# Layer 1 of a two-layer trunk: h as one joined tile per stream, the context's x0 added by DMA, the gate's products in the output projection

## The chip, the cores and the metric

One core of one Trainium2 chip. The time is device microseconds of one execution of the program on that core; the kernel was run three times, and a separate execution was recorded by the hardware profiler. Engines: PE (matrix products), ACT and DVE (elementwise work, also out of PSUM), POOL (elementwise work in SBUF), SP (which here issues all DMAs).

## The reference

Two layers over 256 latent tokens (x) and 256 context tokens (ctx), 2048 features, everything float32. Cut to what matters:

```python
for l in range(2):
    shift, scale, gate = split(silu(c) @ w_mod[l] + b_mod[l], 3)          # for x
    shift_c, scale_c, gate_c = split(silu(c_ctx) @ w_mod[l] + b_mod[l], 3)  # for ctx
    h   = rmsnorm(x, g_pre[l]) * (1 + scale) + shift
    h_c = rmsnorm(ctx, g_pre[l]) * (1 + scale_c) + shift_c
    proj, proj_c = h @ w_in[l], h_c @ w_in[l]        # au av ag q k v bg cx cg
    y = concat(gelu(au) * spatial_mix(gelu(av)) * silu(ag),
               attention(rope(q), [ctx keys, rope(k)], [ctx values, v], sink) * silu(bg),
               (real 2-D DFT of cx, then a linear map) * silu(cg))
    x_new = x + gate * rmsnorm(y @ w_out[l], g_post[l])
    if l == 0:
        ctx = ctx + gate_c * (the same for proj_c, with attention among ctx alone)
    x = x_new
return x
```

In layer 1 the context is used for its keys and values alone; all other products are of the latents.

## The kernel before, in words

**Products.** Every operand of a product is split exactly into a high part in float32r and a low part (operand minus high part), and a product is three matmuls: hi times hi, hi times lo, lo times hi (`mm3`, lines 383 to 386). Weights come in halves of a unit, 128 x 1024 each: SP loads `raw` (three buffers), ACT casts `whi` (L367), DVE subtracts `wlo` (L368), four buffers each; `Stream.next` keeps three halves ahead of PE. The normalised input stands in feature-major tiles, one pair `hh[k]`, `hl[k]` of 128 x 512 per k tile of 128 features: high and low part, columns 0 to 255 the latents (stream 0), 256 to 511 the context (stream 1).

**Units.** `tunit(n)` makes 128 output columns for n tokens: 16 k tiles of three matmuls into one PSUM bank. In layer 0 n is 512, in layer 1 it is 256 (latents only), but for k and v. The order in a layer: av and the first two heads of au together, k tile by k tile (`start_av`, `start_au`), then units au (2), cx (4), ag (4), cg (4), k (2), v, q (8), bg (8); then the output projection, in layer 1 with tokens on partitions, 4 blocks of 512 columns by 16 k tiles by 2 token tiles (`finish`).

**Order of work.** PE runs its instructions in the order of the program. Work that comes back to PE after other engines is written as generators in `Later`: each yields a time to wait, in microseconds of PE's own matmuls, which `tick` counts after every k tile (0.324 for 256 columns, 0.648 for 512, 1.296 for a k tile of the last projection) and checks there; so a wait ends at the next k tile. On the other engines instructions are placed by priority, `low(n)` puts some n places back, and each engine then runs its own list in order. Fourier (`fourier`, waits YF), the spatial mix (`branch_a`), attention (`attention`, waits YQ, YA, YB) and the boundary are such generators.

**Modulation.** Most products of silu(c) and w_mod run on DVE in steps that `pace` gives out per half of a unit: RATE steps per two halves of the phase named. The last 32 steps, `mod_gate1`, are layer 1's gate: four blocks of 512 columns (tiles ctrh, ctrl, nstrh, nstrl), eight steps each, a step being one 512 KB load into `mraw` (two buffers) and two DVE operations (L245, L247), placed behind the newest weights' L368 and at `low(400)`. `gate1`, at the start of the output projection, sums each block over partitions by a matmul with ones (L260) and adds and multiplies rows of b_mod and g_post, loaded into `mraw` as well; `evac` multiplies the projection by it. `turn` brings x1 to tokens on partitions by PE transposes (L847) into the same two PSUM tiles.

**Boundary.** Between the layers `boundary(s, acc)` makes x1 = x0 + gate * y / rms(y) of one stream in place in `yo`, and 1 / rms of x1. For each k tile: DVE multiplies (L933), x0 is added (L934; DVE, or every second time POOL for the latents) from tiles loaded into `raw`, ACT squares (L937), and PE adds the squares over partitions (L944), two or four k tiles at a time. For the latents it runs at the end of layer 0's projection; for the context, within `boundary_ctx`, during layer 1's cx units, followed by the context's h (`make_h`). `gate` overwrites the context's columns of `yo[k]`, so it may not be placed before the context's h of tile k.

Of the kernel before, what the change touches and what calls it, by code (L numbers as in the profile page):

```python
# [27 lines left out]
def units():  # L28
    """(name, first column, columns, first k tile, k tiles): blocks of w_in of 128 x 2048 each."""
# [37 lines left out]
def trunk_kernel(ctx: ExitStack, tc: tile.TileContext, xT, xhalf, cT, wss, wsl, wmod, win, wout0, wout1, const, vec, rows,  # L67
# [24 lines left out]
    # ---- constants  # L92
# [17 lines left out]
    class low:  # L110
        """instructions that may wait for the next `n`."""
# [22 lines left out]
    # ---- modulation: columns [128, 16, stream] of scale, shift and gate  # L134
# [5 lines left out]
    def mod_cols(l, cb, ps8):  # L140
        """ps8 [128, 4, 2]: silu(c) @ w_mod for 512 columns of column block cb."""
# [12 lines left out]
    def mod_start(k0, nk):  # L154
        """scale and shift of k tiles k0 .. k0 + nk - 1 of layer 0 on the tensor engine: yields after
        each unit's products, and before the columns."""
# [39 lines left out]
    def mod_dve(l, cb, red):  # L196
        """red [128, 2, 16]: sums over the 32 partitions of each quadrant, transposed."""
# [38 lines left out]
    def mod_gate1():  # L236
        """products of silu(c) and the gate's columns of w_mod in layer 1, still to be summed over partitions."""
# [16 lines left out]
    def gate1():  # L254
        """(sum + b_mod) * g_post of layer 1's gate, on all partitions."""
        for c in range(4):
            r = sb([P, 2, 512], F32, "mraw", 2)
            DMA.dma_start(r, rows[None, :, c * 512:(c + 1) * 512].to_broadcast([P, 2, 512]))
            ps = ms_ps("gate")
            PE.matmul(ps, ones, g1[c], start=True, stop=True)  # L260
            V.tensor_tensor(out=g1[c], in0=r[:, 0], in1=ps, op=ALU.add)
            V.tensor_tensor(out=g1[c], in0=g1[c], in1=r[:, 1], op=ALU.mult)
            yield YT

    def mod_rest():
# [3 lines left out]
        while "acc" not in state:  # L269
# [6 lines left out]
    YF = [5.0, 2.8], [3.8, 3.4]  # L276
    RATE = dict(au0=2, cx0=2.2, ag0=2.2, cg0=2.2, k0=2, v0=2, q0=1.8, bg0=2.2, out0=2.8,
                k1=2.5, v1=2.5, q1=1, bg1=2.2)
    NEAR = [1] * 6 + [0] * 6 + [1, 2, 3]
    LOWC = 60  # L280
    YT = 2.0
    YH = 2.0
    NX = [4, 2]
    YX, YR = [1.0, 2.0], 0.8
    YQ, YA, YB = [5.5, 6.0], [10.0, 8.0], [3.8, 4.0]

    def pace():
        """steps of the modulation due per half of a unit, behind the latest weights on the vector engine."""
        state["owed"] += RATE.get(state["phase"], 0.0) / 2
        while state["owed"] >= 1:  # L290
            state["owed"] -= 1
            with low(LAG), tc.issue_after(W.last.ins):
                next(mods, None)

    # ---- work of other engines that hands products back to the tensor engine later
# [32 lines left out]
    # ---- weights: raw -> exact parts hi + lo, in halves of a unit, ahead of their use  # L328
# [59 lines left out]
    def part(w, c):  # L388
        """columns c of both parts; a part is a tile or a list of tiles side by side."""
# [19 lines left out]
    # ---- per-token reciprocal rms from sums over features  # L409
# [14 lines left out]
    def col_sums(ps, q, n, start=True, stop=True):  # L424
        """columns of ps: sums over the partitions of q [128, n * 128], one accumulation group."""
# [10 lines left out]
    # ---- streams in feature-major tiles  # L436
# [7 lines left out]

    def make_h(l, k, rb, streams):
        """h = x * rstd * gs + sh, as hi + lo; rb: rstd over the tokens of `streams`."""
# [6 lines left out]
        for s in streams:  # L453
            sl = slice(s * S, (s + 1) * S)
            first = A.activation(hh[k][:, sl], t[:, sl], AF.Identity, bias=sh[l][:, k, s:s + 1])  # L455
        for s in streams:
            sl = slice(s * S, (s + 1) * S)
            last = V.scalar_tensor_tensor(out=hl[k][:, sl], in0=t[:, sl], scalar=sh[l][:, k, s:s + 1],
                                          in1=hh[k][:, sl].bitcast(F32), op0=ALU.add, op1=ALU.subtract)
# [13 lines left out]
    def tunit(n, sl=None):  # L473
        """feature-major product of one unit of 128 columns: PSUM [128, n]."""
# [8 lines left out]
        return ps  # L483

# [10 lines left out]
    # ---- one layer, up to the inputs of the output projection  # L495
    def layer(l):
# [12 lines left out]
        # a_v (token-major) and two heads of a_u, k outermost  # L509
        av = [mm_ps("av") for _ in range(nt)]  # L510
        au = [mm_ps("au") for _ in range(2)]
        def start_av(k, ts):
            c = slice((k % 2) * 512, (k % 2 + 1) * 512)
            for t in ts:
                sl = slice(t * P, (t + 1) * P)
                mm3(av[t], (hh[k][:, sl], hl[k][:, sl]), part(avw, c), k == 0, k == KT - 1)

        def start_au(k):
            for j in range(2):
                c = slice((k % 4) * 256 + j * P, (k % 4) * 256 + (j + 1) * P)  # L520
                mm3(au[j][:, 0:n], part(auw, c), (hh[k][:, 0:n], hl[k][:, 0:n]), k == 0, k == KT - 1)
# [57 lines left out]
        # branch A  # L579
        def branch_a():  # L580
            vt = [w2k([P, 512]) for _ in range(nt)]
            ss = sb([P, 4], F32, "ss")
            for j in range(2):
                A.activation(ytmp(j), au[j][:, 0:n], AF.Gelu_apprx_tanh)
# [20 lines left out]
        # branch C  # L605
# [9 lines left out]
        def fourier(g, ps):  # L615
            """cos(2 pi t m / 256) is even in t around 128 and sin odd: positions t and 256 - t are added for the one
            and subtracted for the other, which leaves 128 rows each (position 128 in the sines' row of t = 0)."""
# [25 lines left out]
        # branch B  # L643
        def rope(hi, lo, ps):
            """x * cos + rot(x) * sin of the latents, and x of the context, as hi + lo."""
# [10 lines left out]
            if hi.shape[-1] > S:  # L656
                split_into(hi[:, CTX], lo[:, CTX], ps[:, S:T])
# [85 lines left out]
        for h in (2, 3):  # L743
            ps = tunit(n)
# [3 lines left out]
        for g in range(4):  # L748
            ps = tunit(n)
# [3 lines left out]
        for h in range(4):  # L753
            ps = tunit(n)
            gate(h, ps)
        state["phase"] = f"cg{l}"
        for g in range(4):
            ps = tunit(n)
# [6 lines left out]
        for j in range(2):  # L765
            ps = tunit(T)
            kt.append((sb([P, T], F32R, f"kt{j}"), sb([P, T], F32R, ("ws", "bsb")[j])))
            rope(*kt[j], ps)
# [3 lines left out]
        for k in range(KT):  # L772
# [3 lines left out]
            for t in range(4):  # L776
                ts = slice(t * P, (t + 1) * P)
                mm3(vps[t][:, 0:256], (hh[k][:, ts], hl[k][:, ts]), part(w, c), k == 0, k == KT - 1)
# [3 lines left out]
        for h in range(8):  # L782
            ps = tunit(n)
# [3 lines left out]
        for h in range(8):  # L787
            ps = tunit(n)
# [11 lines left out]
    # ---- output projection  # L800
# [7 lines left out]
    def out_proj():  # L808
# [14 lines left out]
        later.add(boundary(0, acc), 1.0)  # L823
# [271 lines left out]
```

## Time and profile before

| what | us |
|---|---|
| three runs: median (lowest, highest) | 1170.88 (1170.09, 1171.65) |
| span of the profiled execution | 1167.9 |
| PE busy in it | 1136.0 |
| DVE busy | 881.8 |
| ACT busy | 509.8 |
| POOL busy | 17.3 |

Stages of layer 1 in the profiled execution, read from the order of time: av and au about 757 to 808 us from the span's start, cx with the context's boundary 808 to 845, ag and cg 845 to 893, k and v 893 to 937, q to 1006, bg to 1064, output projection from there. The last product runs at 1158.65; the rest is the last evacuation and the stores.

How to read it: times are microseconds from the start of the span, L944 is line 944 of the kernel. A matmul's duration in the profile runs from its start to its modelled end and overlaps the next one's; its cost in a stream is the distance from start to start. float32 operands (not float32r) take two passes, so such a matmul appears as two. PEld is the load of a matmul's stationary operand. An idle time is put down to the engine or DMA that released it.

### The profile page before, as it was taken

To read this page: it belongs to the slowest core of one execution; us is meant where nothing else is said; L and a number is where in the kernel's file an instruction comes from. 1 tells how busy PE (TensorE), PEld (TensorE's weight loads), DVE (VectorE), ACT (ScalarE), POOL (GpSimd) and SP (SyncE) were. 2 spreads that over 40 slices of the span, in tenths; PEclk is the share of its full clock that TensorE was granted. 3 is DMA by queue.
4 is the path that set the end of the run, shared out by engine and by line. 5 is a ranking of instruction groups with operands and counts; after the bars stand their busy time and mean duration, and the time that the engine had idled before them with its cause. 6 is when DMAs were issued, how large, how long until landed. Compare 5 with 4: busy or idle time off the path is not lost.

```text
span 1167.9 us, 17483 instructions
## 1 busy us (share of the span) xinstructions
PE 1136.0 (97%) x6656; PEld 953.7 (82%) x6656; DVE 881.8 (76%) x1469; ACT 509.8 (44%) x914; POOL 17.3 (1%) x23
## 2 busy tenths in 40 slices
PE   3999999999999999999999999999999999999996
PEld 1466688888898888888888888889899999997885
DVE  5454498888988878798989886495896678888554
ACT  4222513322224667632533233365563278745442
POOL 0000000000000000000000000200000000000001
PEclk9999999999999999999999999999999999999998
DMA  9999765466665334455466665365656665688563
GB/s 339 378 387 357 254 196 166 145 202 193 200 200 178 105 114 136 134 175 173 158 199 209 205 216 162 109 207 173 205 158 205 203 200 178 195 269 244 190 187 120
DMA packets 73892, 234.32 MB, mean 201 GB/s; under 512 B 8528, under 2 KB 9680, under 8 KB 73808
## 3 DMA queue, kind: packets, MB, share of 16 engines
q1 hardware_dynamic: 73808, 233.21, 61.6%
q8 instruction: 52, 0.85, 0.3%
q14 instruction: 32, 0.26, 0.1%
HBM read 231.08 MB, written 2.10 MB: 200 GB/s over the span
## 4 chain that ended last, share of the span: by engine, by line
PE 92%; DVE 3%; DMA 2%; ACT 2%; issue 1%; POOL 0%; SPq 0%; DVEq 0%; ACTq 0%; POOLq 0%
PE ps_t L384 20%; PE ps_t L385 20%; PE ps_t L386 20%; PE ps_mod L172 3%; PE ps_av L384 2%; PE ps_y L386 2%; PE ps_y L384 2%; PE ps_y L385 2%; PE ps_av L385 2%; PE ps_av L386 2%; PE ps_v L386 1%; PE ps_v L384 1%; PE ps_v L385 1%; PE ps_tp L722 1%; PE ps_au L384 1%
## 5 line engine op out<-in xcount | busy, mean ns | idle before, releaser
L384 PE MATMUL ps_t<-hh,whi 128*128 128x512 f32 (+1 forms) x1296 | 452.1, 349 | 0.0
L386 PE MATMUL ps_t<-hh,wlo 128*128 128x512 f32 (+1 forms) x1296 | 447.4, 345 | 0.0
L385 PE MATMUL ps_t<-hl,whi 128*128 128x512 f32 (+1 forms) x1296 | 447.0, 345 | 0.0
L367 ACT CAST whi<-raw 128x1024 fp32r<-128x1024 f32 x218 | 228.2, 1050 | 397.3 <-PE ps_t L385 274.4
L368 DVE TENSOR_TENSOR wlo<-raw,whi 128x1024 fp32r<-128x1024 f32 x218 | 265.3, 1220 | 99.1 <-ACT whi L367 98.8
L384 PEld LDWEIGHTS ps_t<-hh,whi 128*128 128x128 f32 x1296 | 244.9, 189 | 34.3 <-issue 4.6
L386 PEld LDWEIGHTS ps_t<-hh,wlo 128*128 128x128 f32 x1296 | 244.7, 189 | 30.6
L385 PEld LDWEIGHTS ps_t<-hl,whi 128*128 128x128 f32 x1296 | 244.9, 189 | 28.9 <-issue 0.5
L209 DVE SCALAR_TENSOR_TENSOR macc<-mraw,cs,macc 128x512 f32<-128x512 f32 x360 | 249.9, 745 | 17.6 <-DMA mraw<-in_wmod_dram 17.5
L455 ACT ACTIVATE hh<-w2k,sh 128x256 fp32r<-128x256 f32 x64 | 29.0, 502 | 61.4 <-DVE w2k L451 61.4
L384 PE MATMUL ps_y<-whi,hh 128*128 128x512 f32 x112 | 45.0, 401 | 0.0
L386 PE MATMUL ps_y<-whi,hl 128*128 128x512 f32 x112 | 43.8, 392 | 0.0
L385 PE MATMUL ps_y<-wlo,hh 128*128 128x512 f32 x112 | 43.7, 390 | 0.0
L384 PE MATMUL ps_av<-whi,hh 128*128 128x512 f32 x96 | 40.0, 416 | 0.0
L385 PE MATMUL ps_av<-wlo,hh 128*128 128x512 f32 x96 | 37.9, 395 | 0.4 <-DVE wlo L368 0.4
L172 PE MATMUL ps_mod<-hh,kt 128*32 128x512 f32 x64 | 21.5, 649 | 17.0 <-DMA hh<-in_wss_dram 17.0
L386 PE MATMUL ps_av<-whi,hl 128*128 128x512 f32 x96 | 37.6, 392 | 0.0
L386 PE MATMUL ps_v<-whi,hl 128*128 128x256 f32 x128 | 36.2, 283 | 0.0
L384 PE MATMUL ps_v<-whi,hh 128*128 128x256 f32 x128 | 36.2, 283 | 0.0
L385 PE MATMUL ps_v<-wlo,hh 128*128 128x256 f32 x128 | 36.2, 283 | 0.0
L468 DVE TENSOR_TENSOR acc<-acc,w2k 128x512 f32<-128x512 f32 (+1 forms) x33 | 21.2, 641 | 18.7 <-ACT w2k L467 17.2
L401 ACT CAST w2k<-ps_tp 128x512 fp32r<-128x512 f32 x40 | 23.5, 587 | 22.8 <-PE ps_scc L385 12.0
(292 smaller groups left out, 1491.8 us busy)
## 6 DMA issues: line engine op xcount, KB each, us to landing
raw<-in_win_dram SPq DMA_DIRECT2D x160, 512.0 KB, 4.1
mraw<-in_wmod_dram SPq DMA_DIRECT2D x128, 512.0 KB, 4.3
raw<-in_wout_dram SPq DMA_DIRECT2D x64, 512.0 KB, 4.2
hh<-in_wss_dram SPq DMA_DIRECT2D x32, 256.0 KB, 5.6
hl<-in_wss_dram SPq DMA_DIRECT2D x32, 256.0 KB, 5.4
yo<-in_xT_dram SPq DMA_DIRECT2D x16, 256.0 KB, 5.4
mraw<-in_wsl_dram SPq DMA_DIRECT2D x8, 512.0 KB, 6.9
yo<-in_wsl_dram SPq DMA_DIRECT2D x16, 256.0 KB, 7.2
```

The source lines that it names most:

```text
L172: PE.matmul(ps[32 * kk:32 * kk + 32, 0:n], cpad[:, kg * 4 + kk], ws[kk], start=kg == 0, stop=kg == 3, tile_position=(0, 32 * kk))
L209: V.scalar_tensor_tensor(out=acc[:, s], in0=w[:, kk % 2], scalar=c, in1=acc[:, s], op0=ALU.mult, op1=ALU.add)
L367: A.copy(ph, r[:, c])
L368: self.last = V.tensor_tensor(out=pl, in0=r[:, c], in1=ph.bitcast(F32), op=ALU.subtract)
L384: PE.matmul(ps, st[0], mv[0], start=start, stop=False)
L385: PE.matmul(ps, st[0], mv[1], start=False, stop=False)
L386: PE.matmul(ps, st[1], mv[0], start=False, stop=stop)
L401: A.copy(hi, src)
L455: first = A.activation(hh[k][:, sl], t[:, sl], AF.Identity, bias=sh[l][:, k, s:s + 1])
L468: V.tensor_tensor(out=acc[:, sl], in0=acc[:, sl], in1=q[:, sl], op=ALU.add)
L722: PE.transpose(tp[:, (2 * j + b) * P:(2 * j + b + 1) * P], src, ident)
```

## The change

In layer 1 each stream's high and low parts of h stand side by side in one tile (`hh[k]` the latents, `hl[k]` the context), so that w_hi is applied to both in one matmul of 512 columns and w_lo to the high part in one of 256; the two halves of the PSUM bank are then added by ACT and DVE (`joined`), and what follows reads the sum from SBUF. k takes this form for both streams, one product each; av and v keep three matmuls, on slices of the new tiles.

The context's boundary becomes a function of its own: x0 is added by a DMA on POOL's queue that accumulates into `yo[k]`, the squares are summed over k on DVE, and the sum over partitions is made once by `col_sums`, as for the first rms. The waits of Fourier in layer 1 are longer (YF).

Gate's products slow down in bg and go on in the output projection (RATE), `gate1` waits for each block, its rows go to the tiles ws and bsb, and it and `turn` run at other intervals (YT, YG). The products themselves are the same. Comments and docstrings are dropped as well; those lines are not shown.

```diff
-    YF = [5.0, 2.8], [3.8, 3.4]
+    YF = [5.0, 2.8], [6.0, 5.2]
     RATE = dict(au0=2, cx0=2.2, ag0=2.2, cg0=2.2, k0=2, v0=2, q0=1.8, bg0=2.2, out0=2.8,
-                k1=2.5, v1=2.5, q1=1, bg1=2.2)
+                k1=2.5, v1=2.5, q1=1, bg1=0.3, out1=1.4)
-    YT = 2.0
+    YT, YG = 3.0, 6.0
-    NX = [4, 2]
-    YX, YR = [1.0, 2.0], 0.8
+    NX, LATE = 4, 6
+    YX, YR, YC, YE = 1.0, 0.8, 1.1, 3.5
...
     def gate1():
         for c in range(4):
-            r = sb([P, 2, 512], F32, "mraw", 2)
-            DMA.dma_start(r, rows[None, :, c * 512:(c + 1) * 512].to_broadcast([P, 2, 512]))
+            while len(g1) <= c:
+                yield 1.0
+            r = [sb([P, 512], F32, tag) for tag in ("ws", "bsb")]
+            for i in range(2):
+                DMA.dma_start(r[i], rows[None, i, c * 512:(c + 1) * 512].to_broadcast([P, 512]))
             ps = ms_ps("gate")
             PE.matmul(ps, ones, g1[c], start=True, stop=True)
-            V.tensor_tensor(out=g1[c], in0=r[:, 0], in1=ps, op=ALU.add)
-            V.tensor_tensor(out=g1[c], in0=g1[c], in1=r[:, 1], op=ALU.mult)
-            yield YT
+            V.tensor_tensor(out=g1[c], in0=r[0], in1=ps, op=ALU.add)
+            V.tensor_tensor(out=g1[c], in0=g1[c], in1=r[1], op=ALU.mult)
+            state["gates"] = c + 1
+            yield YG
...
+    def h_of(l, k, sl):
+        if l == 0:
+            return hh[k][:, sl], hl[k][:, sl]
+        s, a = sl.start // S, sl.start % S
+        t, b = (hh, hl)[s][k], a + sl.stop - sl.start
+        return t[:, a:b], t[:, S + a:S + b]
...
+    def mm2(ps, w, h, k):
+        PE.matmul(ps, w[0], h, start=k == 0, stop=False)
+        PE.matmul(ps[:, 0:S], w[1], h[:, 0:S], start=False, stop=k == KT - 1)
+
+    def joined(ps):
+        t = sb([P, S], F32, "join", 2)
+        A.copy(t, ps[:, S:T])
+        V.tensor_tensor(out=t, in0=t, in1=ps[:, 0:S], op=ALU.add)
+        return t
+
+    def tunit1(streams):
+        pss = [mm_ps("t") for _ in streams]
+        for k in range(KT):
+            if k % 8 == 0:
+                w = W.next()
+            for s, ps in zip(streams, pss):
+                mm2(ps, part(w, slice((k % 8) * P, (k % 8 + 1) * P)), (hh, hl)[s][k], k)
+                later.tick(PASS * S)
+        return [joined(ps) for ps in pss]
...
         def start_au(k):
             for j in range(2):
                 c = slice((k % 4) * 256 + j * P, (k % 4) * 256 + (j + 1) * P)
-                mm3(au[j][:, 0:n], part(auw, c), (hh[k][:, 0:n], hl[k][:, 0:n]), k == 0, k == KT - 1)
+                if last:
+                    mm2(au[j], part(auw, c), hh[k], k)
+                else:
+                    mm3(au[j], part(auw, c), (hh[k], hl[k]), k == 0, k == KT - 1)
...
-            ps = tunit(n)
+            ps = tunit1([0])[0] if last else tunit(n)
...
-            ps = tunit(T)
+            pss = tunit1([0, 1]) if last else [tunit(T)]
             kt.append((sb([P, T], F32R, f"kt{j}"), sb([P, T], F32R, ("ws", "bsb")[j])))
-            rope(*kt[j], ps)
+            rope(*kt[j], *pss)
...
         later.add(gate1(), YT)
-        later.add(turn(), 2 * YT)
+        later.add(turn(), 1.5 * YT)
+        state["phase"] = "out1"
...
+    def rms_of(s, acc, wait):
+        ps = ms_ps("rs")
+        col_sums(ps, acc, 2)
+        dg = rstd_diag(ps[:, 0:2], 2, D)
+        yield wait
+        return bcast(dg, 2)[:, 0:S]
...
+    def boundary_ctx(acc):
+        r = sb([P, S], F32, "rbs", 2)
+        r0 = yield from rms_of(1, acc[:, CTX], 3.2)
+        A.copy(r, r0)
+        acc1 = acc[:, CTX]
+        for k in range(KT + LATE):
+            if k < KT:
+                V.tensor_tensor(out=yo[k][:, CTX], in0=yo[k][:, CTX], in1=r, op=ALU.mult)
+                G.dma_start(yo[k][:, CTX], xhalf[1, k // 4][:, k % 4], accum_op=ALU.add)
+            i = k - LATE
+            if i >= 0:
+                q = w2k([P, S]) if i else acc1
+                A.activation(q, yo[i][:, CTX], AF.Square)
+                if i:
+                    V.tensor_tensor(out=acc1, in0=acc1, in1=q, op=ALU.add)
+            if k % 2:
+                yield YC
+        yield YE
+        r0 = yield from rms_of(1, acc1, 4.0)
+        r = sb([P, S], F32, "rbs", 2)
+        V.tensor_copy(r, r0)
+        for i, k in enumerate(ORDER):
+            make_h(1, k, r, [1])
+            state["ctx"].append(k)
+            if i % 2:
+                yield YH
...
     def after_start(l):
         if l == 1:
-            later.add(boundary_ctx())
+            later.add(lowered(boundary_ctx(state["acc"])))
```

`boundary` keeps the latents' case alone (with NX = 4 and YX = 1.0 as before). `lowered` runs a generator at `low(100)`, as before, now around all of `boundary_ctx`.

## The prediction

> **What bounds the kernel now.** I read the page first (busy shares, chain), then the busy time by stretches of the span, then the order of time on each engine around the edits. PE is busy for 97% of the span and holds 92% of the chain that ended last, at a granted clock of 1.00 in every stretch below. So the cost of an edit is the PE time it adds or removes, plus any wait it puts in front of PE.
>
> ```profile
> PE 1136.0 (97%) x6656; PEld 953.7 (82%) x6656; DVE 881.8 (76%) x1469; ACT 509.8 (44%) x914; POOL 17.3 (1%) x23
> PE 92%; DVE 3%; DMA 2%; ACT 2%; issue 1%; POOL 0%; SPq 0%; DVEq 0%; ACTq 0%; POOLq 0%
> 808.00:845.00 37.00, 37.00 (x294) 32.59 (x293) 28.61 (x67) 20.30 (x47) 1.03 (x2) 1.00 0.59 185
> 937.00:1006.00 69.00, 67.71 (x528) 65.25 (x527) 55.84 (x101) 54.85 (x109) 0.00 (x0) 1.00 0.58 183
> 1006.00:1064.00 58.00, 57.40 (x468) 56.43 (x468) 52.04 (x84) 33.17 (x63) 0.00 (x0) 1.00 0.80 254
> 1064.00:1153.00 89.00, 87.92 (x392) 70.29 (x392) 49.13 (x64) 40.67 (x60) 0.00 (x0) 1.00 0.57 180
> ```
>
> The last four lines are windows: length, then busy time (and count) of PE, PEld, DVE, ACT, POOL, then clock, DMA share, GB/s. In order: layer 1's cx units with the context's boundary; the q units with attention; the bg units with the rest of attention and half of the gate's products; the output projection. DVE is at 77%, 81%, 90% and 55% there: the spare room is in the last.
>
> **Part 1: joined h (mm2 for mm3).** Per k tile a layer-1 unit makes three 256-column matmuls now; it will make one of 512 and one of 256, the same columns with one matmul fewer. The order of time where av (512) and au (256) alternate gives the spacing:
>
> ```profile
> 775.92 0.39 PE L386 MATMUL ps_av<-whi,hl 128*128 128x512 f32 x1
> 776.14 0.28 PE L384 MATMUL ps_au<-hh,whi 128*128 128x256 f32 x1
> 776.26 0.28 PE L385 MATMUL ps_au<-hl,whi 128*128 128x256 f32 x1
> 776.38 0.28 PE L386 MATMUL ps_au<-hh,wlo 128*128 128x256 f32 x1
> ...
> 776.74 0.28 PE L386 MATMUL ps_au<-hh,wlo 128*128 128x256 f32 x1
> 776.86 0.39 PE L384 MATMUL ps_av<-whi,hh 128*128 128x512 f32 x1
> ```
>
> The durations overlap; what counts is start to start: 0.12 us for 256 columns, 0.22 to 0.23 for 512, and a 256 before a 512 still takes 0.12. Over longer stretches 11 k tiles of 256 columns take 3.95 us (877.87 to 881.82), 0.1197 per matmul, and 512 columns take 0.2267. Doubling the columns thus does not double the time; each matmul carries about 0.0127 us beside its columns. A k tile goes from 0.3591 to 0.2267 + 0.1197 = 0.3464. There are 30 one-stream units of 16 k tiles (2 au, 4 cx, 4 ag, 4 cg, 8 q, 8 bg) and 2 au heads of 16, 512 in all: 512 x 0.0127 = **-6.5 us**. The two k units run both streams and go from 3 x 0.2267 to 2 x 0.3464 per k tile: 32 x 0.0127 = **+0.4**. av and v keep their shapes. Bounds: -6.5 if every merge pays as measured, 0 if a long-short alternation saves nothing; I take the first, as the alternating rows above show it.
>
> The Trainium skill (TensorE: Matmul & The Clock Gate, The mechanism) says that a weight load overlaps running matmuls only when the row groups differ; by its figure of P / 1.2, some 107 ns a load (LDWEIGHTS section), 512 loads fewer would be worth an estimated 55 us. The trace disagrees: the load of a full-height tile starts with the matmul before it (PEld at 877.87 and 877.99, as PE's), and 0.12 us has no room for a load outside it.
>
> What it adds: joined() is one ACT copy and one DVE add of 128x256 for each of 36 products (0.37 to 0.38 us on ACT as L926, 0.42 on DVE as L934), 13.5 and 15 us over layer 1. PE covers it where its consumers have slack. fourier is given longer waits. In q the chain has little: one head's rotation starts at 975.25, its low part ends at 982.02, and PE asks for it at 984.23, so 2.2 us, of which the join with its two handovers takes some 1.0. Bounds 0 to 8 x 0.5; I take **+0.5** in q, where ACT and DVE rise to about 86% and 88%.
>
> **Part 2: the context's boundary.** It loses the 16 column-sum matmuls of L944 (their partner x0 adds and the row copy L948 too).
>
> ```profile
> 814.13 0.28 PE L386 MATMUL ps_t<-hh,wlo 128*128 128x256 f32 x1
> 814.34 0.63 PE L944 MATMUL ps_rs<-w2k,ones 128*32 128x256 f32 x4
> 814.90 0.38 PE L384 MATMUL ps_t<-hh,whi 128*128 128x256 f32 x1
> ```
>
> One pair (x4: two passes each) opens 0.77 us between neighbours that stand 0.12 apart: 0.65 us, eight times, **-5.2 us**. Instead PE runs col_sums a second time (808.12 to 808.71, 0.59) for L952 (843.31 to 843.67, 0.36): **+0.2**. On DVE 16 x0 adds become 15 square adds, no change. Also gone are four 512 KB x0 loads through SP's queue and three raw buffers; PE waited for no weights there, so that is worth nothing.
>
> New are 16 accumulating DMAs on POOL's queue, one behind each multiply. No DMA of POOL's and no accumulation is in this trace. Behind POOL's issue stand only its own later issues and one power per rms; behind the landing stand ACT's square, and in ACT's order the weights' casts, then DVE's add, then PE's col_sums. The time allowed: boundary starts about 807.3; wait 3.2 is ten k tiles, so multiplies begin about 812; a 1.1 wait rounds up to four ticks of 0.324, four k tiles or 1.39 us; 11 such waits and 11 k tiles for the 3.5 are 55 x 0.3464 = 19.1, and about 4.5 us of mixing and Fourier matmuls lie between. PE asks at about 835.4, ACT's and DVE's last piece takes 0.85: 16 issues and one landing have 22 us. Issue lies between SP's 0.33 and the longest POOL step among these rows, 1.04 (746.30, x3 in 3.12); landing between 1.9 (128 KB out) and 6.3 (64 KB const): 7 to 23 us, so the stall is 0 to 1. I take **+0.4**. Casts run three halves (8.3 us) ahead, which covers ACT's own wait of up to 3 us; without that cover the same wait would stand in front of PE once.
>
> **Part 3: gate's products.** Steps done by the end of bg, with 0.8 carried over from before: 10 in k and v, 8 in q, then at 2.2 per two halves the rest of the 32, at 0.3 only 2.4, 21.2 in all. So 11 steps move, each two L247 (0.75 us) and one 512 KB load: 16.5 us of DVE and 5.8 MB leave a stage at 90%. They go to the output projection: the same 16.5 us, into a stage where DVE is idle for 40. SP's queue takes their loads between weights; there DMA share goes from 0.57 to about 0.7, below the 0.80 that bg ran at without PE stopping for weights.
>
> Waits now: PE's ps_x L847 waited 1.1 us for gate 0 and 2 (one mraw buffer, rows landing in 6.1 us), ps_o L385 1.7 us for L402 behind L247, only 0.4 of it after 1006. With rows in ws and bsb, and gates 6.0 apart, I take **-1.1** and **-0.4**. But gate 3 is late next: with 21.2 and 0.7 per half, step 32 falls at the 16th half of it, c = 1, k = 14, and the gate's matmul follows one k tile later, since gate1 looks every 1.0. Its products stand behind the newest weights:
>
> ```profile
> 1106.92 1.05 ACT L367 CAST whi<-raw 128x1024 fp32r<-128x1024 f32 x1 [1.75 <-PE ps_y L386]
> 1108.00 1.23 DVE L368 TENSOR_TENSOR wlo<-raw,whi 128x1024 fp32r<-128x1024 f32 x1 [1.57 <-ACT whi L367]
> ```
>
> ACT's cast is released by PE's half, DVE ends 2.3 us into it, two L247 end 3.8 us in; PE arrives 1.37 us in: **+2.4** (bounds 0, if the order by priority lets them run earlier, and 6.4 with a 4 us load in front).
>
> **Sum**, on the profiled 1167.9: -6.5 + 0.4 + 0.5 - 5.2 + 0.2 + 0.4 - 1.1 - 0.4 + 2.4 = -9.3, so 1158.6. The runs' median, 1170.9, stands 3.0 above the span; the forecast is **1161.6 us**, with its own range 1156 to 1165.
>
> **Rivals.** (a) Slower: POOL's issues starve. Evidence for: each would run among DVE operations that read two tiles from SBUF, and POOL's L934 stretched from 0.79 to 1.04 among them. If each issue waits out a 1.22 us wlo beside its 1.04, 16 x 2.26 + 4.1 + 0.85 = 41 us against 23.4 (812 to 835.4): PE stalls 17.7 us, time 1179. It decides from 16x + 4.1 = 22 + 9.7, x = 1.7 us an issue. Against: L934's rows among DVE's were mostly 0.79. The Trainium skill (SBUF — State Buffer, SBUF: two separate sides) states that DVE in a two-port mode locks POOL out of writing descriptors, and infers that two-input adds do not; no run here shows either. Chance 0.17. (b) Attention becomes the bound in q: each of 8 heads loses 0.8 us more to ACT and DVE, 6 us, 1168. For: 81% DVE already with waits on L402; against: 2.2 us of slack. Chance 0.12. (c) The merge does not do what it says: the 256 after a 512 costs the 0.0127 back, 1168. Against: the alternating rows. Chance 0.06. The forecast keeps 0.65.
>
> **How the numbers follow.** 0.2% (2.3 us) is about what a measurement can tell from no change. Faster by more: all of the forecast, half of (b) and (c): 0.74. Within: the other half of those less a tail, 0.08. Slower: (a) and that tail, 0.18. Range: forecast, (b) and (c) hold 0.83, so 1156 to 1170.
>
> **What would show it.** Right: L944 down to 32 passes; 256 and 512 columns alternating at 0.347 a k tile; the cx stretch about 6 us shorter; POOL issues under 1.1 us. Wrong: PE waiting before the second col_sums by over 2 us, 0.36 per k tile, waits on ps_sc in q, or a gate wait in the output projection of other than about 2.4 us.

## The result

| kernel | median us (lowest to highest, runs) | ratio to before, 95% interval | profiled span |
|---|---|---|---|
| before, in the same job | 1171.1 (1170.1 to 1171.7, 4) | | 1167.9 |
| changed | 1180.7 (1177.2 to 1181.6, 4) | 1.0076 [1.0061, 1.0091] | 1179.8 |

The forecast was 1161.6 with a range of 1156 to 1170: wrong in sign, and outside its range. The page of the changed kernel has PE busy for 1 us less than before and the span 12 us longer, so the loss is not in PE's work; DMA has gone from 2% to 3% of the chain that ended last.

```profile
PE 1134.9 (96%) x6146; PEld 932.6 (79%) x6146; DVE 896.0 (76%) x1503; ACT 521.4 (44%) x950; POOL 31.0 (3%) x39
PE 92%; DMA 3%; DVE 2%; issue 1%; POOL 1%; ACT 1%; SPq 0%; DVEq 0%; ACTq 0%; POOLq 0%
```

Where it went is read by following the same PE instructions through both traces (the first of each stage's group), and taking the difference of their times, changed minus before:

| stretch | difference, us |
|---|---|
| the span's start to av's start (layer 0, which the change leaves alone) | +0.6 |
| to the first broadcast of the context's rms | +0.4 |
| to the second broadcast (context's boundary, cx) | +4.4 |
| to v's start (ag, cg, k) | -0.7 |
| to the last product of attention (q, bg) | -4.3 |
| to the first product of the projection | -0.3 |
| to its last product | +12.3 |
| to the end | -0.5 |

The waits of PE name the places. Columns: total, times, longest, in us.

```profile
PE ps_gate L263 <- DVE nstrh L247: 6.9, 1, 6.9
PE ps_rs L433 <- DVE acc L1017: 5.3, 1, 5.3
PE ps_gate L263 <- DVE nstrl L247: 2.6, 1, 2.6
PE ps_z L390 <- DVE w2k L406: 1.3, 2, 0.9
```

L433 is the second `col_sums` of the context's boundary, L263 the sum of gate's products (nstrh is gate 2, nstrl gate 3). The windows show what else they cost (columns as before: PE, PEld, DVE, ACT, POOL, clock, DMA share, GB/s):

```profile
808.00:838.00 30.00, 28.30 (x169) 24.48 (x167) 23.80 (x55) 17.98 (x41) 15.16 (x17) 1.00 0.92 211
838.00:846.00 8.00, 2.95 (x13) 2.86 (x14) 6.27 (x17) 3.15 (x9) 0.76 (x1) 0.62 0.42 131
846.00:893.00 47.00, 47.00 (x265) 41.28 (x265) 38.05 (x71) 28.37 (x52) 0.00 (x0) 0.96 0.47 146
937.00:1006.00 69.00, 68.99 (x423) 61.17 (x422) 59.44 (x112) 56.52 (x117) 0.00 (x0) 1.00 0.61 193
1006.00:1060.00 54.00, 54.00 (x334) 48.17 (x333) 39.03 (x63) 34.96 (x69) 0.00 (x0) 1.00 0.56 174
...
1080.00:1100.00 20.00, 13.11 (x48) 9.75 (x47) 11.85 (x15) 5.68 (x11) 0.00 (x0) 0.74 0.75 263
...
1120.00:1140.00 20.00, 17.41 (x69) 13.31 (x68) 10.81 (x12) 7.19 (x10) 0.00 (x0) 0.91 0.49 145
```

Around each of the three longest waits the granted clock falls below 1.00, and matmuls start at half the rate. In cx this costs (1 - 0.96) x 47 = 1.9 us, and half of the 2.95 busy us in 838 to 846 = 1.5, together 3.4, beside the wait of 5.3. In the projection PE runs at half the rate from 1090.26 to 1095.85 and from 1123.52 to 1126.57; half of these 8.6 us, 4.3, is lost. With the waits of 9.5 that makes 13.8; the stretch is only 12.3 longer, because the new handling of the gates also saves there (1.8 by itself, below). In q, PE is now busy for all of 69 us, with DVE and ACT at 86% and 82%; in bg DVE has fallen from 90% to 72%.

The second lateness, followed instruction by instruction. Order of time of the changed kernel, around the gate's matmul:

```profile
1078.84 0.33 SPq L261 DMA_DIRECT2D bsb<-in_rows_dram  x1
1079.26 2.80 SPq L362 DMA_DIRECT2D raw<-in_wout_dram  x2
1082.11 0.43 SPq L243 DMA_DIRECT2D mraw<-in_wmod_dram  x1
1088.67 1.54 DVE L247 SCALAR_TENSOR_TENSOR nstrh<-mraw,cs,nstrh 128x512 f32<-128x512 f32 x2 [4.10 <-DMA mraw<-in_wmod_dram]
1090.26 2.08 PE L263 MATMUL ps_gate<-nstrh,ones 128*128 128x512 f32 x2 [6.89 <-DVE nstrh L247]
...
1093.85 0.63 PE L390 MATMUL ps_y<-whi,hl 128*128 128x512 f32 x1
1094.27 0.63 PE L388 MATMUL ps_y<-whi,hh 128*128 128x512 f32 x1
...
1096.38 0.40 PE L388 MATMUL ps_y<-whi,hh 128*128 128x512 f32 x1
1096.62 0.39 PE L389 MATMUL ps_y<-wlo,hh 128*128 128x512 f32 x1
```

SP issues in the order of its list. The load of gate 2's last product (1082.11) stands behind weight loads that wait for a free buffer, and behind gate 2's rows (1076.9 and 1078.8), whose tiles are free only when gate 1 is done. It lands some 6.5 us after its issue, and DVE finishes the block 6.9 us after PE asks for it. After that wait 512-column matmuls start 0.43 us apart, and 0.23 apart from 1095.9 on.

The first lateness, in cx, again in order of time:

```profile
833.57 0.41 DVE L1010 TENSOR_TENSOR yo<-yo,rbs 128x256 f32<-128x256 f32 x1
833.60 1.77 POOL L1011 DMA_DIRECT2D yo<-in_xhalf_dram  x2 [2.12 <-DVE yo L1010]
837.48 0.28 PE L431 MATMUL ps_rs<-zero,ones 128*128 128x2 f32 x2
841.67 1.32 DVE L1017 TENSOR_TENSOR acc<-acc,w2k 128x256 f32<-128x256 f32 x3
843.05 1.01 PE L433 MATMUL ps_rs<-ones,acc 128*128 128x1 f32 x4 [5.29 <-DVE acc L1017]
```

The last multiply (L1010) is at 833.57 where the forecast's times put it near 824, and PE asks at 837.5 (835.4 forecast). The last two pieces of x0 land 3.6 and 3.9 us after their issue, the later one at 838.20. ACT's last squares then end at 839.74, and DVE's last adds, which stand behind weights and Fourier's work in its list, at 842.99: 4.8 us after the last landing. Two DMA queues share the engines in 805 to 846 (packets, MB, share of 16 engines), and ACT waits for landings:

```profile
q1 hardware_dynamic: 1586, 5.77, 44.8%
q0 software_dynamic: 2304, 2.10, 34.4%
```

```profile
ACT w2k L1015 <- DMA yo<-in_xhalf_dram: 3.9, 5, 1.9
ACT acc L1015 <- DMA yo<-in_xhalf_dram: 2.5, 1, 2.5
```

Per MB the accumulating queue takes 16.4% of the engines against 7.8% for the weights' queue, and its landing takes 3.6, 7.3 and 10.1 us (least, median, most). These count from the start of an issue's record, and POOL's issues queue behind one another; from the end of the issue the landing takes 2.7, 5.4 and 7.3 us.

### The profile page after: what moved, and what is told of

The parts are those of the page before. It is cut to its first block, busy times and chain, and to the rows that moved or that the text cites. A ratio compares the mean times of both kernels' runs of the same rounds, so it can differ in the third digit from the quotient of the medians.

```text
span 1179.8 us, 16577 instructions
## 1 busy us (share of the span) xinstructions
PE 1134.9 (96%) x6146; PEld 932.6 (79%) x6146; DVE 896.0 (76%) x1503; ACT 521.4 (44%) x950; POOL 31.0 (3%) x39
## 4 chain that ended last, share of the span: by engine, by line
PE 92%; DMA 3%; DVE 2%; issue 1%; POOL 1%; ACT 1%; SPq 0%; DVEq 0%; ACTq 0%; POOLq 0%
PE ps_t L388 15%; PE ps_t L389 15%; PE ps_t L390 15%; PE ps_t L500 10%; PE ps_t L501 5%; PE ps_mod L172 3%; PE ps_av L388 2%; PE ps_y L388 2%; PE ps_y L390 2%; PE ps_y L389 2%; PE ps_av L389 2%; PE ps_av L390 2%; PE ps_tp L763 1%; PE ps_v L390 1%; PE ps_v L388 1%; PE ps_v L389 1%
## 5 line engine op out<-in xcount | busy, mean ns | idle before, releaser
L388 PE MATMUL ps_t<-hh,whi 128*128 128x512 f32 (+1 forms) x784 | 301.0, 384 | 0.0
L390 PE MATMUL ps_t<-hh,wlo 128*128 128x512 f32 (+1 forms) x784 | 299.4, 382 | 0.0
L389 PE MATMUL ps_t<-hl,whi 128*128 128x512 f32 (+1 forms) x784 | 299.1, 382 | 0.0
L500 PE MATMUL ps_t<-hh,whi 128*128 128x512 f32 x512 | 187.1, 403 | 0.0
L389 PEld LDWEIGHTS ps_t<-hl,whi 128*128 128x128 f32 x784 | 147.4, 188 | 27.3 <-issue 0.2
L501 PE MATMUL ps_t<-hh,wlo 128*128 128x256 f32 x512 | 144.1, 281 | 0.0
L467 ACT ACTIVATE hh<-w2k,sh 128x256 fp32r<-128x256 f32 x48 | 21.7, 502 | 56.6 <-DVE w2k L463 56.6
```

The costliest lines, as they stand in the source:

```text
L388: PE.matmul(ps, st[0], mv[0], start=start, stop=False)
L389: PE.matmul(ps, st[0], mv[1], start=False, stop=False)
L390: PE.matmul(ps, st[1], mv[0], start=False, stop=stop)
L467: first = A.activation(h_of(l, k, sl)[0], t[:, sl], AF.Identity, bias=sh[l][:, k, s:s + 1])
L500: PE.matmul(ps, w[0], h, start=k == 0, stop=False)
L501: PE.matmul(ps[:, 0:S], w[1], h[:, 0:S], start=False, stop=k == KT - 1)
```

## The experiments

Times are medians; each ratio is to the kernel before in the same job (1171.1 to 1172.6).

| kernel | us | ratio [95%] |
|---|---|---|
| joined h alone | 1176.1 | 1.0038 [1.0023, 1.0053] |
| boundary by DMA alone | 1173.9 | 1.0020 [1.0010, 1.0030] |
| gate's products alone | 1176.4 | 1.0041 [1.0027, 1.0056] |
| changed, gate's products back in bg | 1167.2 | 0.9955 [0.9940, 0.9969] |
| changed, gates 2 and 3 asked later | 1166.0 | 0.9958 [0.9944, 0.9972] |
| products back, x0 added by POOL | 1171.5 | 1.0002 [0.9993, 1.0012] |
| products back, old boundary | 1164.1 | 0.9940 [0.9925, 0.9955] |
| products back, boundary not put back in priority | 1165.2 | 0.9945 [0.9928, 0.9963] |
| products back, x0 by plain DMA | 1163.8 | 0.9934 [0.9917, 0.9950] |
| products back, squares ten k tiles behind | 1164.2 | 0.9939 [0.9923, 0.9955] |
| gates' new handling alone | 1167.1 | 0.9961 [0.9948, 0.9974] |
| old boundary, gates 2 and 3 later | 1162.8 | 0.9925 [0.9912, 0.9938] |
| products back, boundary two units sooner | 1161.8 | 0.9911 [0.9896, 0.9926] |
| boundary sooner, gates 2 and 3 later | 1160.7 | 0.9904 [0.9887, 0.9921] |
| the same, first broadcast later | 1159.8 | 0.9898 [0.9882, 0.9915] |

**Each part alone.** First the three parts, each put into the kernel before by itself.

Joined h alone (`h_of`, `mm2`, `joined`, `tunit1`, YF; old boundary, old gates):

> Part 1 alone (joined h; the context's boundary and gate's products as in the kernel before). Theory: each of the 512 merges saves 0.0127 us of PE as its rows show, k gives 0.4 back, the joins cost PE at most 0.5: 1171 - 6 = about 1165 us, 0.346 us a k tile. Rival: the ACT copy and DVE add of each product make attention and Fourier late, and PE's waits in q and bg take the gain: 1168 to 1171 us, with new waits on ps_sc, ps_o or ps_z of 3 us or more.

```profile
PE ps_x L884 <- DVE ctrh L261: 9.9, 1, 9.9
```

```profile
1057.97 10.77 SPq L358 DMA_DIRECT2D raw<-in_wout_dram  x4
1070.18 1.95 SPq L258 DMA_DIRECT2D mraw<-in_rows_dram  x2
```

Neither. q and bg gained 3.0 us, but the projection lost 10.2: one wait of 9.9 for gate's rows. In SP's order of time four weight loads now stand ahead of the rows' loads and wait for buffers; before, the rows went at 1054.2 and 1058.3, ahead of them. The kernel with the same joined h and the rows in ws and bsb (old boundary, below) has no such wait, so the matmuls' form is not what makes it. Why SP's list came out in another order here is not shown.

Boundary by DMA alone (three matmuls per k tile, old gates, Fourier's shorter waits of before):

> Part 2 alone (x0 added by accumulating DMAs on POOL's queue, squares summed on DVE; h and gate's products as before). Theory: PE loses 5.2 us of column sums, but the DMAs land 5 to 10 us after issue, ACT's list stops at their squares, and PE waits 3 to 6 us for the last of the sum, then runs about 2 us more at a lower granted clock: 1171 + 0 to 4 us = 1171 to 1175 us. Rival: the wait comes of the joins' extra work on ACT and DVE in the same stretch: then none here, and 1166 us.

The stretch between the two broadcasts was 2.6 us longer than before, of which 2.2 came back by v. The time is the theory's, the mechanism is not: there is no wait at the sum here. The waits are spread over Fourier (ps_f 1.9 and 0.8, ps_z 1.7 and 0.6), and the clock is 1.00 in all windows from 808 to 893. So the boundary's new work makes ACT and DVE late without any join, and the 5 us of column sums are spent on it: from av's start to v the kernel is 1.5 us longer than before.

Gate's products alone (`gate1`, RATE, YT, YG):

> Part 3 alone (gate's products slowed in bg and made in the output projection; h and boundary as before). Theory: PE asks for gates 2 and 3 before DVE has their last products: waits of about 7 and 2.6 us and some 3 us at a lower clock, 1.5 us saved in attention and at the old gates: 1171 + 11 = 1182 us. Rival: the waits come of PE reaching the projection faster with joined h: under 3 us of waits, 1173 us.

Waits of 3.7 (gate 2) and 2.6 (gate 3), and 6.6 us lost in the projection: so the loss belongs to this part by itself, and gate 3's wait is close to the forecast's 2.4. The clock fell to half for 3.41 us behind gate 2's wait and not at all behind gate 3's. Gate 2's 3.7 is less than the 6.9 of the changed kernel, where q and bg are shorter and PE asks 4.4 us sooner after v.

**The gates.** Two ways of taking the lateness away, both in the changed kernel:

```diff
-                k1=2.5, v1=2.5, q1=1, bg1=0.3, out1=1.4)
+                k1=2.5, v1=2.5, q1=1, bg1=2.2)
```

> The changed kernel with part 3's rates undone alone (2.2 steps in bg, none in the projection; gate1's rows in ws and bsb, its intervals and turn's as changed). Theory: the projection's stretch loses its 12.3 us, bg gets back waits of about 1 us: 1181 - 11 = 1170 us. Rival: the late gates come of the rows' loads standing in SP's queue between weights, whatever the rates: then gate waits of 5 us or more remain and the time stays above 1176 us.

```diff
             while len(g1) <= c:
                 yield 1.0
+            if c > 1:
+                yield YL
...
-    YT, YG = 3.0, 6.0
+    YT, YG, YL = 3.0, 6.0, 14.0
```

> The changed kernel, where gate1 waits 14 us of PE's own time more before it asks for gates 2 and 3 (both are needed only at the ends of the third and fourth block). Theory: PE asked too early; the waits of 6.9 and 2.6 us in the projection and the 4 us at a lower clock behind them go, 1181 - 13 = 1168 us. Rival: the product loads stand in SP's list behind weight loads that wait for PE, so PE finds them late whenever it asks: waits of 5 us or more remain, above 1176 us.

Both remove the gates' waits wholly: the projection takes 1.8 us less than before in each, in place of 12.3 more. With the products left in the projection, q and bg gain 4.3 us; with the products back in bg 2.4 here, and 2.4 to 3.8 in the seven kernels of the table that have them back. So the move is worth 0.4 to 1.9 us, if gates 2 and 3 are asked for late enough. The ratios of these two kernels, 0.9955 and 0.9958, do not tell them apart.

**The gates' new handling by itself.** Rows in ws and bsb, gates 6 us apart; nothing else of the change:

> The kernel before with only the new handling of the gates in the projection (rows in the tiles ws and bsb, 6 us between gates, the transposes at 3 us steps); three matmuls per k tile, old boundary, all of gate's products in bg. It is the partner of the run with the old boundary (1164.1), which differs from it by the joined h alone. Theory (a merged pair saves 0.010 us, 512 of them 5 us, and the joins cost little): this run takes 1168.5 to 1169.5, so joined h by itself is worth 4.5 to 5.5 us. Rival (most of that run's gain came from the gates' new handling, and the merge is worth under 3 us): this run takes under 1167.

1167.1, between the two. In the trace it is 1.8 us in the projection. Its partner with joined h (old boundary, below) gains 4.2 us from av's start to the last product, this one 2.0, so joined h (with Fourier's longer waits, which belong to it) is worth 2.2 us net; by the medians' ratios it is 0.0021 of 1171, 2.5 us, and the two intervals overlap a little. That is the rival's size for the merge.

The reason stands in the k tiles. Order of time of the changed kernel, 512 and 256 columns alternating:

```profile
814.88 0.39 PE L500 MATMUL ps_t<-hh,whi 128*128 128x512 f32 x1
815.11 0.27 PE L501 MATMUL ps_t<-hh,wlo 128*128 128x256 f32 x1
815.23 0.40 PE L500 MATMUL ps_t<-hh,whi 128*128 128x512 f32 x1
815.46 0.28 PE L501 MATMUL ps_t<-hh,wlo 128*128 128x256 f32 x1
```

Start to start a k tile takes 0.35 here; over 407 k tiles of the kernel with old boundary the mean is 0.3572 against 0.3640 for 410 k tiles of before. So a merge is worth 0.0067, not 0.0127: the 512 takes 0.23 to 0.24 in the alternation, where 512s among themselves take 0.2267. k's two units pay the other way: a k tile takes 0.706 for two products in place of 0.684 for one.

**The sum in cx: what makes it late.** All of these have gate's products back in bg (sum waited for 6.1 us there).

x0 loaded by SP and added by POOL in place of the DMA:

```diff
-                G.dma_start(yo[k][:, CTX], xhalf[1, k // 4][:, k % 4], accum_op=ALU.add)
+                G.tensor_tensor(out=yo[k][:, CTX], in0=yo[k][:, CTX], in1=x0s[k // 4][:, k % 4], op=ALU.add)
```

> Gate's products back in bg (as in gates_back) and the context's x0 loaded by SP into raw buffers and added by POOL, in place of the accumulating DMAs; the sum of squares stays on DVE. Theory: the accumulating DMAs land late and ACT's list stops at their squares, so without them the wait before the second column sums falls from 6.1 to under 2 us and the clock stays up: 1167 - 4 - 3 = 1160 us. Rival: DVE's list, which holds the adds back behind weights and Fourier work, makes the wait: it stays at 5 us or more, 1167 us.

Neither number: 1171.5. The wait fell to 3.8, but ps_z (2.3) and ps_f (1.7) waited instead. The multiplies of DVE, with their least, median and most ns, first in this kernel, then in the changed one:

```profile
L1020 DVE TENSOR_TENSOR yo<-yo,rbs x16: 406/423/965, 812.2 to 837.1; 128x256 f32<-128x256 f32 x16
```

```profile
L1010 DVE TENSOR_TENSOR yo<-yo,rbs x16: 406/418/422, 813.7 to 833.6; 128x256 f32<-128x256 f32 x16
```

While POOL adds, DVE's multiplies, which read two tiles from SBUF, take up to more than twice as long; beside POOL's DMA issues they stay as they are.

The boundary of before (L944's column sums, x0 added by DVE):

> Gate's products back in bg, and the context's boundary as in the kernel before (x0 loads, DVE adds, column sums on PE); joined h and gate1's new tiles and intervals stay. Theory: the 6.1 us wait and about 3.4 us at a lower clock go, 5.0 us of column sums return: 1167 - 9.5 - 1.9 + 5.9 = 1162 us. Rival: the stretch is bound by ACT and DVE either way and PE waits elsewhere in it: 1167 us.

1164.1, between the two numbers, but with the theory's mechanism. No wait is left in cx, and the stretch between the broadcasts is as long as before (+0.2). So what the new boundary saves on PE it costs again in waits, and more.

Boundary at normal priority:

```diff
-            later.add(lowered(boundary_ctx(state["acc"])))
+            later.add(boundary_ctx(state["acc"]))
```

> Gate's products back in bg, and the context's boundary (with its accumulating DMAs) run at the usual priority in place of 100 places back. Theory: the DMAs' landing is what is late, so the order changes little: the wait stays at 4 us or more, 1165 to 1168 us. Rival: DVE's and ACT's order is what holds the squares and adds back: the wait falls under 2 us, 1160 us.

The theory's time, 1165.2, and its wait. The wait fell from 6.1 to 4.2 and ps_z came up with 1.4; ACT still waited 6.7 us for landings. Order accounts for some 2 us.

Plain DMA in place of the accumulating one:

```diff
-                G.dma_start(yo[k][:, CTX], xhalf[1, k // 4][:, k % 4], accum_op=ALU.add)
+                G.dma_start(yo[k][:, CTX], xhalf[1, k // 4][:, k % 4])
```

> As the run with gate's products back in bg (1167.2, PE waits 6.1 us for the context's sum), but POOL's 16 DMAs write x0 over the tile in place of adding to it; so the context's x1 lacks gate * y / rms(y). Issue, queue, bytes and order stay. Theory (the accumulation itself makes the landing late: median 7.3 us, up to 10.1, and twice the DMA engines' time per byte of plain loads): landing falls to 2 to 4 us, ACT no longer waits for landings, the wait for the sum is at most 3 us, and the time is 1162 to 1164. Rival (POOL's issue of 0.87 to 0.9 us each and the shared DMA engines set the pace, whatever the transfer does): wait 5 to 6 us, time within 1 us of 1167.

Its queue in 805 to 846, and issue to landing:

```profile
q0 software_dynamic: 768, 2.10, 14.6%
```

```profile
DMA to landing us min/median/max: 2.5/3.6/5.4
```

The transfer behaved as the theory said (share 34.4% to 14.6%, landing 7.3 to 3.6, issue 0.87 to 0.55), and the time came to 1163.8 as it said, but the wait is still 4.2, not under 3. The last multiply is at 831.3, hardly sooner, in a DVE that is busy for 26.8 of the 30 us before 838.

Squares ten k tiles behind:

```diff
-    NX, LATE = 4, 6
-    YX, YR, YC, YE = 1.0, 0.8, 1.1, 3.5
+    NX, LATE = 4, 10
+    YX, YR, YC, YE = 1.0, 0.8, 1.1, 0.9
```

> As the run with gate's products back in bg, but each square is placed ten k tiles behind its multiply (six before), and the last wait shortened from 3.5 to 0.9 so that PE asks for the sum at about the same time. Theory (ACT's list stops at squares whose x0 has not landed, which holds the weights' casts, then DVE's list and so the last multiplies and POOL's last issues, 827 to 834 in place of 824): with the squares later ACT waits under 2 us for landings, the multiplies end by about 827, the wait for the sum falls from 6.1 to 2 to 3 us and the time to 1162 to 1164. Rival (the landing of the last piece itself is the length of the wait): the last multiplies end earlier but the wait stays at 4 us or more, time 1165.5 or over.

The last multiply moved to 829.4 and the time to 1164.2, yet the wait is 4.7: the rival's wait with the theory's time. DVE is at 26.7 of 30 us here too. So landing and order each hold the sum back; no run eases both in the same place. In both runs DVE is the fuller engine, busy for 89% of the 30 us before 838, ACT for 64 and 63%.

**More time for the same work.** The boundary starts before the last two au units, squares ten k tiles behind, PE asking at nearly the same place:

```diff
+        after_start(l)
         for h in (2, 3):
             ps = tunit1([0])[0] if last else tunit(n)
             A.activation(ytmp(h), ps[:, 0:n], AF.Gelu_apprx_tanh)
-        after_start(l)
```

> As the run with squares ten k tiles behind (1164.2, wait 4.7), but the context's boundary begins before the last two au units, some 11 us of PE sooner, and PE asks for the sum at nearly the same place (the last wait is 11.0 in place of 0.9). Theory (the wait and the low clock behind it are the whole loss; the column sums' 5.2 us are saved underneath): no wait for the sum, granted clock 1.00 through cx, the stretch from the first broadcast of the rms to the h of the context shorter than before's by 4 to 6 us, time 1156.5 to 1159.5. Rival (ACT and DVE are full in au and cx: the same work only moves the delay to the spatial mix or to Fourier): waits of 2 us or more at ps_mix, ps_f or ps_z take the place of the one for the sum, time 1161 or over.

1161.8, within the rival's time and not the theory's, though none of the rival's waits came. The sum is not waited for any more, and the clock is 1.00 from 808 to the last product. From Fourier's matrices to v the kernel is 2.4 us shorter than before; the forecast of 4 to 6 is missed by one other wait, at the first broadcast:

```profile
801.52 0.70 PE L437 MATMUL ps_rb<-w2k,ones 128*128 128x256 f32 x2 [1.84 <-DVE mgl L406]
801.87 0.63 PE L500 MATMUL ps_t<-hh,whi 128*128 128x512 f32 x1
...
805.07 0.63 PE L500 MATMUL ps_t<-hh,whi 128*128 128x512 f32 x1
805.50 0.36 PE L501 MATMUL ps_t<-hh,wlo 128*128 128x256 f32 x1
805.70 0.39 PE L500 MATMUL ps_t<-hh,whi 128*128 128x512 f32 x1
```

It waits for DVE to read Fourier's matrices out of a PSUM tile that it needs, and the six k tiles behind it take 0.64 each in place of 0.35: 1.8 us of wait, and 6 x 0.29 = 1.7 more of clock. By these numbers the stretch would be 5.9 shorter than before without that wait; this is an estimate, and no run here reaches it.

**Together.** Old boundary with gates 2 and 3 later (the edit delays these two, and not every gate as the expectation has it); then the earlier boundary with them:

> This run takes together what the runs so far left standing: joined h, the context's boundary as before (column sums per pair, x0 added by DVE), and gate's products in the output projection with every gate asked for 14 us later. Theory: the parts are independent, so it keeps the 1164.1 of the run with the old boundary and the gate's products in bg, plus the relief of q and bg that moving the products gives (there the stretch from v to the first projection block shortened by 4.1 us against 1.2 to 2.8 with the products in bg): about 1162.5, with no wait of PE before a gate product and none of over 1 us in cx. Rival: the later gates hold back the tail of the projection, or the products' loads meet the weights' loads there, so that what bg gains is given back: 1164 to 1166.

The theory's number: 1162.8, and no wait of PE over 0.5 us in layer 1. Earlier boundary:

> The changed kernel with both its late places given time: context's boundary begun two units earlier with squares ten k tiles behind, and gates 2 and 3 asked for 14 us later. Theory (the three parts of the forecast are additive once nothing is waited for): the run above less 1.2 to 1.6 for q and bg, 1155 to 1158, which is the forecast's sum or below. Rival (the parts share DVE and DMA, and one gives back what the other gains): 1159 or over.

1160.7, the rival's number and not the theory's 1155 to 1158. But q and bg gain 4.3 us and the projection 1.8, as they do without the earlier boundary, so these parts add; the wait of 1.8 at the first broadcast is in this run too. Asking for that 3 us later:

```diff
-        r0 = yield from rms_of(1, acc[:, CTX], 3.2)
+        r0 = yield from rms_of(1, acc[:, CTX], 6.2)
```

> As the run with all parts placed earlier (1160.7, span 1158.3), but PE asks for the first broadcast of the context's rms 6.2 us after its sum in place of 3.2, and the last wait before the squares' sum is 8.0 in place of 11.0. Theory (what is missing is the wait of 1.8 us at the first broadcast and the lower clock for some 4 us behind it, worth another 2 us): no wait of PE over 0.5 us from the spatial mix to the end, granted clock 1.00 in that stretch, and 3 to 4 us less: 1156.7 to 1157.7. Rival (ACT and DVE are what holds the stretch, and the wait moves on to the sum or to Fourier): 1160 or over.

```profile
PE ps_f L390 <- DVE w2k L639: 2.0, 1, 2.0
```

The rival's mechanism: the wait moved on to Fourier, with the clock at 0.94 from 808 to 838. Its 1159.8 cannot be told from the run before it. This version is 1.0% faster than the kernel before and some 1.8% faster than the changed one. What stays open is whether any placement in cx avoids the last 2 us of wait; none here did with this boundary.

## Why the prediction was wrong, by its own steps

- **The wait for the DMA and the sum, "+0.4": this is the first step that failed.** The forecast counted 16 issues and one landing on POOL's queue against 22 us, 0.85 for the last piece on ACT and DVE, and took both engines as free before it. The issues were right (0.87 alone, eleven in a row in 10.07, within 0.33 to 1.04 each), and so were the last two landings (3.6 and 3.9, within 1.9 to 6.3); most landings before them were longer, 7.3 in the median. What failed is the part of ACT and DVE. The last multiply came at 833.6 and not near 824, and the last piece took 4.8 us from landing to last add (838.20 to 842.99) and not 0.85. The place of the squares in the lists has a share in the first: the last multiply comes at 829.4 with squares ten k tiles behind, against 832.9 in the kernel that differs by this and the last wait alone. The three halves by which casts run ahead did cover the weights, for which PE waits nowhere in cx, but not these operations. In place of 0.4 stood 5.3 at the sum, 1.3 at Fourier and 3.4 of clock. In the run with the boundary two units sooner the sum is no longer waited for; that all of the saving of -5.2 is there underneath is the estimate above and not shown. The plain DMA and the late squares show that landing and order each carry a part.
- **"Gate 3 is late next": right, and not enough: the second step that failed.** The forecast had the projection 1.3 us longer (2.4 less 1.1); it was 12.3. Gate 3's wait was 2.6 (2.4 forecast). Gate 2 was taken to be in time; its loads stood behind weight loads and rows in SP's list, 6.9 us. The forecast said that SP takes these loads "between weights", and did not ask when SP's list gets to them.
- **No term for the clock.** The sum took a wait as its own length. Here waits of 2.6 to 6.9 us brought 3.4 us in cx and 4.3 in the projection on top.
- **The merge, -6.5, mis-sized.** A merge is worth 0.0067, so the term is 512 x 0.0067 = 3.4; k costs 32 x 0.022 = 0.7, not 0.4. The failed step is the one that added 0.2267, a price of 512s among themselves, to 0.1197. A k tile in alternation takes 0.3572 where 0.347 was forecast.
- **Joins in q, +0.5, and no attention bound (rival b): right.** PE waits nowhere in q. q and bg gained 4.3 us where the sum had some 3 (256 merges of 0.0127, less the joins, and the 0.4 wait). By the measured 0.0067 the merges are 1.7. Most of the rest is idle time of PE that is gone: before, it was busy for 67.71 of 69 us in q and 57.40 of 58 in bg, so idle for 1.9, of which the forecast counted 0.4. The remaining 0.7 stays open.
- **Old gate waits, -1.1: right in place and short in size.** The new handling by itself gives 1.8 in the projection.
- **Rival (a), POOL's issues starved, 1179:** near the time and not the cause. Eleven issues in a row took 0.92 each beside DVE's operations, where one alone took 0.87, and DVE's multiplies ran at their usual 0.418 beside them; that the time came near is luck. **Rival (c), the merge saves nothing:** half true, 0.0067 of the 0.0127.

## What to carry to other kernels

A wait of the engine that bounds the kernel is priced by its length and, if it fills enough of one window of the clock (next section), by the slower clock behind it. If a change moves work off that engine, the first question is whether the engines that take it over finish before it asks, with every in-order list between them walked through, the DMA issuer's too. Where a producer is late, asking later or starting sooner is often one number in the schedule, and worth trying before the change is judged. Try each part of a joint change alone and with its late places mended: here each part alone made the kernel 0.2 to 0.4% slower, and all three, with their late places given time, make it 1.0% faster.

## What the runs showed of the hardware that was not expected

- The granted clock is either 1.00 or 0.50 in these traces, and its slow stretches last 3.41, 6.83 or 10.24 us, on a grid that is fixed within one execution. In them matmuls of 512 columns start 0.43 us apart, behind them 0.23. What tells the cases apart is how long PE is idle within one window of that grid, and not how long a wait is. In all 17 traces, from 60 to 1145 us, a window at 1.00 with up to 1.75 us idle was followed by 1.00, and one with 1.81 us or more by 0.50. So a wait of 1.84 within one window halved the clock (products back, boundary two units sooner), and one of 2.6 across two did not (gate's products alone). Two windows of each, in this order, with PE busy in the second column and the clock behind POOL's:

```profile
798.85:802.26 3.41, 1.56 (x7) 0.95 (x6) 3.22 (x4) 0.83 (x2) 0.00 (x0) 1.00 0.30 101
802.26:805.67 3.41, 3.41 (x12) 2.88 (x11) 2.44 (x7) 0.94 (x2) 2.25 (x4) 0.50 0.69 233
...
1116.71:1120.13 3.42, 1.67 (x6) 1.09 (x7) 2.10 (x4) 0.00 (x0) 0.00 (x0) 1.00 0.68 218
1120.13:1123.54 3.41, 3.41 (x17) 2.80 (x16) 3.13 (x5) 2.31 (x5) 0.00 (x0) 1.00 0.05 20
```

The Trainium skill (TensorE: Matmul & The Clock Gate, Part 1: The HAM clock gate) describes a gate that passes half the pulses after an idle window of about 3.4 us, watched by a free-running counter. The half rate and the length of the window agree; that the window must be idle as a whole does not, as a little more than half of it was enough here.

- An accumulating DMA of 128 KB on POOL's queue took 0.87 us to issue and 7.3 to land in the median (5.4 from the end of its issue), the same transfer without accumulation 0.55 and 3.6 (3.0 from the end of its issue), and 34.4% against 14.6% of the DMA engines' time in that stretch.
- Additions on POOL lengthened DVE's multiplies from 0.418 to as much as 0.965 us; POOL's DMA issues did not.
